# Storing the few first keys at both ends of a key row, one transpose fewer per attention head, and two moves in TensorE's order

## The chip, the cores and the metric

The kernel runs on one core of a Trainium2 chip. Its time is the device time of one execution in microseconds. The kernel before took 1043.29 us, the median of three runs from 1043.16 to 1043.96.

## The reference

One decoder layer over 16 meta tokens and 256 tokens (272 in all) of width 2048, in float32. One product gives eight attention queries of width 128, a shared key and value latent of width 256, sixteen indexer queries of width 64 with one indexer key, and 1024 pooling channels.

```python
score = jnp.einsum('bqhs,bqh->bqs', jax.nn.relu(dots), wi).astype(jnp.float32)
...
_, sel = lax.top_k(score, top_k)
...
logits = jnp.einsum('bqhc,bqkc->bhqk', qa, c_sel).astype(jnp.float32) * (HEAD_DIM ** -0.5)
...
p = jax.nn.softmax(logits, axis=-1).astype(c_sel.dtype)
```

The indexer's score picks the 64 best admissible keys of each query; logits get a relative bias, and the softmax's weights sum the values of those keys. Beside it, four groups of the pooling channels get trailing means over 2, 4, 8 and 16 tokens, less the token, and a small product. Both halves go through one output product, a layer norm, a gated feed-forward part with a short convolution, and a second layer norm.

## The kernel before

TensorE does nearly all of its products in three passes: each float32 operand is split into an upper part in the chip's rounded float32 form and a lower part, and upper times upper, upper times lower and lower times upper are summed (L199 to L201 for the projections). ScalarE makes the upper part of each weight tile (L127), VectorE the lower (L128), SyncE's queue brings the tiles, two ahead.

The 256 queries stand in two blocks of 128. The first block looks at keys 0 to 143 (`KA` = 144), the second at all 272 (`KB`); the two sets lie side by side in rows of `KW` = 416. In both, the 16 meta keys come first. They are the "few first keys", handled apart from the 128 or 256 others: their values are a separate tile `v0` (L419), in which the rows of an upper part, a lower part and the upper part again start at partitions 0, 32 and 64, with cleared rows between.

The order of the work before the output product is this:

1. TensorE warms up on a cleared tile with 13 small products (L86 to L89), then makes indexer keys, weights and latent (L268 to L270).
2. Eight weight tiles make the indexer's queries, a pair of heads each. The pair before is multiplied with the indexer keys in between (`dots`, L352); ScalarE applies the relu (L361, L362) and VectorE adds it to `score` (L364).
3. The key heads (L394 to L401): six products each into one of four PSUM buffers `at`, which `small()` hands out in turn, evacuated by ScalarE (L401). The indexer's last pair is issued behind the third of the eight heads and uses the same buffers.
4. The values (L421 to L438): meta keys first, through `few` (L409), then the two other blocks.
5. The top-k on VectorE (L444 to L448), a comparison that marks the keys left out (L450), and eight updates of the bias (L452). Meanwhile TensorE makes the eight query heads (L456 to L460).
6. The head loop (L585). Each turn computes one tile of pooling channels in 16 groups of three matmuls and puts the attention in between: behind group 4 the logits of the next head (`softmax`), behind group 7 the values of the head before (`values`), behind group 9 the transposes of this head's softmax (`turn`). `turn` makes five transposes: three of 128 keys and, of the two blocks' meta keys, two of 16. `ptx`, the turned weights of the meta keys, is a cleared tile into which ScalarE and VectorE copy upper, upper and lower parts (L514 to L520). Behind the tile, ScalarE evacuates it to `u` (L549), GpSimd adds 4, 4, 3, 3, 2, 2, 1 and 1 times for the window sums (L553), and VectorE takes the token off (L559) in the next turn.

The framework orders each engine's instructions by its own scheduling, within what the program's dependences leave; pools with few buffers make an instruction wait for the reader of the buffer before. After the loop come the output product, the norm and the feed-forward part, which the change doesn't touch.

Of the kernel before, what the change touches and what calls it, by code (L numbers as in the profile page):

```python
# [11 lines left out]
F32 = mybir.dt.float32  # L12
# [5 lines left out]
P = 128  # L18
D = 2048
NM = 16  # L20
# [48 lines left out]
def tile_layer(ctx, tc, xt, w_first, w_proj, w_uk, w_uv, w_pool, w_o, w_up, w_down, cols, rows, rel_bias, onehot, out):  # L69
# [16 lines left out]
    nc.gpsimd.memset(warm, 0.0)  # L86
    ps = small()
    for _ in range(13):
        nc.tensor.matmul(ps[:, :256], warm[:, :P], warm, start=True, stop=True)  # L89


# [200 lines left out]
    ct = kt[:, H - 2:, :]  # L292
    sqs = []
    for j in range(2):
        ps = heads[1 + j][0]
# [37 lines left out]
    def relative_bias():  # L333
        rb_sb = temp([32, H], "rb_sb")
        nc.sync.dma_start(rb_sb, rel_bias)
        oh = temp([32, T], "oh")
        nc.sync.dma_start(oh, onehot)
        ps = small()
        nc.tensor.matmul(ps[:H, :T], rb_sb, oh, start=True, stop=True)
        strip = temp([H, STRIP], "strip")  # L340
        nc.vector.memset(strip, NEG)
        nc.vector.tensor_copy(strip[:, P:], ps[:H, :T])
        strip_d = dram.tile([H, STRIP], F32, name="strip_d")
        nc.gpsimd.dma_start(strip_d, strip)
        for dst, n_rows, t0, n in ((bias[:, :, :KB], P, NM + P, KB), (bias[:, :, KB:], P, NM, KA), (bias_m, 2, Q0, NM)):

            src = bass.AP(tensor=strip_d.tensor, offset=strip_d.offset + P + t0 - (n - 1),
                          ap=[[1, n_rows], [STRIP, H], [1, n]])
            nc.gpsimd.dma_start(dst, src)


    def dots(j, qi, pa_, heads):  # L352

        for i in heads:
            h = 2 * j + i
            pb = small()
            for o, n, t in ((pa_[:, S * i:S * i + S], S, slice(0, P)), (pb[:, :T], T, slice(P, S))):
                nc.tensor.matmul(o, qi[:, i, t], kidx[:, 0, :n], start=True, stop=False)  # L358
                nc.tensor.matmul(o, qi[:, i, t], kidx[:, 1 + i, :n], start=False, stop=True)
# [34 lines left out]
    for h in range(H):  # L394
        ps = small()
        for c in range(2):
            w = slice(1024 * c + h * HD, 1024 * c + h * HD + HD)
            nc.tensor.matmul(ps[:, :T], uk[:, 0, w], ctp[:, c, 0, :], start=c == 0, stop=False)
            nc.tensor.matmul(ps[:, :T], uk[:, 0, w], ctp[:, c, 1, :], start=False, stop=False)
            nc.tensor.matmul(ps[:, :T], uk[:, 1, w], ctp[:, c, 0, :], start=False, stop=c == 1)  # L400
        nc.scalar.activation(kt[:, h, :], ps[:, :T], AF.Copy)  # L401
# [12 lines left out]
    for i, (a, b) in enumerate(((0, NM), (NM, NM + P), (NM + P, T))):  # L414
        if i:
            v = ap_.tile([b - a, 1024], F32, name=f"v{i}", tag=f"v{i}")
        else:

            v = ap_.tile([80, 1024], F32R, name="v0")  # L419
            nc.gpsimd.memset(v.bitcast(F32), 0.0)  # L420
        for g in range(2):  # L421
            ps = small()
            for c in range(2):
                w = slice(1024 * c + 512 * g, 1024 * c + 512 * g + 512)
                if i == 0:
                    nc.tensor.matmul(ps[:48], few[:, c, :], uv[:, 0, w], start=c == 0, stop=False)
                    nc.tensor.matmul(ps[:48], few[:, c, :], uv[:, 1, w], start=False, stop=c == 1)
# [12 lines left out]


# [2 lines left out]
    for r in range(TOPK // 8):  # L444
# [2 lines left out]
            nc.vector.max(m8, src[:, a:b])  # L447
            nc.vector.match_replace(out=work[:, a:b], in_to_replace=m8, in_values=src[:, a:b], imm_value=REPLACED)  # L448
        src = work
    nc.vector.tensor_tensor(work, work, score, op=ALU.is_equal)  # L450
    for h in range(H):
        nc.vector.scalar_tensor_tensor(bias_of(h), work, NEG, bias_of(h), op0=ALU.mult, op1=ALU.add)  # L452


    qt = ap_.tile([P, H, NQ], F32, name="qt", tag="q")
# [11 lines left out]
    lm = ap_.tile([2, H, NM], F32, name="lm")  # L467
# [9 lines left out]
    pm_sb = ap_.tile([NM, H, 2], F32, name="pm_sb")  # L477

    def meta_weights():
        pmeta = small()  # L480
        for h in range(H):
            nc.tensor.transpose(pmeta[:NM, 2 * h:2 * h + 2], lm[:, h, :], ident[:2, :2])
        nc.vector.tensor_copy(pm_sb.rearrange("p a b -> p (a b)"), pmeta[:NM, :2 * H])


    mix = [None] * KT
    AB = ((0, KA), (KA, KW))

    def softmax(h):
        ps = big()  # L490
        nc.tensor.matmul(ps[:, :KA], qt[:, h, 2:2 + P], kt[:, h, :KA], start=True, stop=True)
        nc.tensor.matmul(ps[:, KA:KW], qt[:, h, 2 + P:], kt[:, h, :], start=True, stop=True)
        lg = temp([P, KW], "lg")
        nc.vector.scalar_tensor_tensor(lg, ps[:, :KW], scale, bias_of(h), op0=ALU.mult, op1=ALU.add)
        st = ap_.tile([P, 3, 2], F32, name="st", tag="st", bufs=2)
        for i, (a, b) in enumerate(AB):
# [3 lines left out]
        for i, (a, b) in enumerate(AB):  # L500
            nc.vector.tensor_scalar_mul(lg[:, a:b], lg[:, a:b], st[:, 2, i:i + 1])
        return lg

    def turn(h, lg):
        pt, ptm = small(), small()
        nc.tensor.transpose(pt[:, :P], lg[:, NM:KA], ident)
        nc.tensor.transpose(pt[:, P:2 * P], lg[:, KA + NM:KA + NM + P], ident)
        nc.tensor.transpose(pt[:, 2 * P:3 * P], lg[:, KA + NM + P:], ident)
        nc.tensor.transpose(ptm[:NM, :P], lg[:, :NM], ident)
        nc.tensor.transpose(ptm[:NM, P:2 * P], lg[:, KA:KA + NM], ident)  # L510
        pts = temp([P, 3 * P], "pts")
        nc.scalar.activation(pts, pt[:, :3 * P], AF.Copy)

        ptx = ap_.tile([80, NQ], F32R, name="ptx", tag="t", bufs=4, padded_shape=[P, KW])  # L514
        nc.gpsimd.memset(ptx.bitcast(F32), 0.0)
        for r in (0, 32):
            nc.vector.tensor_copy(ptx[r:r + NM, :2], pm_sb[:, h, :])
            nc.scalar.activation(ptx[r:r + NM, 2:], ptm[:NM, :2 * P], AF.Copy)
        nc.vector.tensor_tensor(ptx[64:64 + NM, :2], pm_sb[:, h, :], ptx[:NM, :2].bitcast(F32), op=ALU.subtract)
        nc.vector.tensor_tensor(ptx[64:64 + NM, 2:], ptm[:NM, :2 * P], ptx[:NM, 2:].bitcast(F32), op=ALU.subtract)  # L520
        return pts, ptx

    def values(h, pts, ptx):
# [61 lines left out]
    for h in range(H):  # L585
# [498 lines left out]
```

## Time and profile before

| | |
|---|---|
| median of three runs | 1043.29 us |
| the profiled execution | 1043.2 us |
| its span, first to last instruction | 1041.3 us |
| granted TensorE clock, mean | 0.998 |
| TensorE, VectorE, ScalarE, GpSimd busy | 1033.3, 891.0, 621.0, 189.5 us |
| DMA, mean | 240 GB/s |

A row of the timeline has the start in microseconds from the span's start, the time that the row takes, the engine (PE is TensorE, PEld its weight loads, DVE VectorE, ACT ScalarE, POOL GpSimd, SP SyncE), the line of the kernel, the operation, what it writes and what it reads, and a count where equal neighbours are put together. In square brackets stands the idle time of the engine ahead of it with what ended that. Matmuls are pipelined: one row lasts longer than the step to the next, so the steps between starts are what tell.

### The profile page before, as it was taken

To read this page: it belongs to the slowest core of one execution; us is meant where nothing else is said; L and a number is where in the kernel's file an instruction comes from. 1 tells how busy PE (TensorE), PEld (TensorE's weight loads), DVE (VectorE), ACT (ScalarE), POOL (GpSimd) and SP (SyncE) were. 2 spreads that over 40 slices of the span, in tenths; PEclk is the share of its full clock that TensorE was granted. 3 is DMA by queue.
4 is the path that set the end of the run, shared out by engine and by line. 5 is a ranking of instruction groups with operands and counts; after the bars stand their busy time and mean duration, and the time that the engine had idled before them with its cause. 6 is when DMAs were issued, how large, how long until landed. Compare 5 with 4: busy or idle time off the path is not lost.

```text
span 1041.3 us, 19198 instructions
## 1 busy us (share of the span) xinstructions
PE 1033.3 (99%) x7643; PEld 984.3 (95%) x7643; DVE 891.0 (86%) x1401; ACT 621.0 (60%) x1000; POOL 189.5 (18%) x246
## 2 busy tenths in 40 slices
PE   9999999999999999999999999999999999999997
PEld 9999999999999999999999999999999999999986
DVE  6879568758779998888999999989998999999876
ACT  7656446645439855555665556555556565565665
POOL 1200014125330021130121111211112101120031
PEclk9999999999999999999999999999999999999999
DMA  9755543354553578879887788877988778887865
GB/s 326 259 187 218 214 142 131 134 200 165 176 189 131 197 223 240 278 282 302 274 277 261 269 297 276 276 263 267 296 271 285 264 274 285 279 273 271 288 215 160
DMA packets 59754, 250.28 MB, mean 240 GB/s; under 512 B 21734, under 2 KB 22416, under 8 KB 32656
## 3 DMA queue, kind: packets, MB, share of 16 engines
q1 hardware_dynamic: 34592, 230.42, 61.2%
q0 software_dynamic: 7888, 16.14, 8.3%
q10 hardware_dynamic: 17184, 2.49, 1.4%
q8 instruction: 60, 0.98, 0.4%
q14 instruction: 30, 0.25, 0.1%
HBM read 232.50 MB, written 2.11 MB: 225 GB/s over the span
## 4 chain that ended last, share of the span: by engine, by line
PE 89%; DVE 5%; issue 3%; ACT 1%; POOL 1%; DMA 1%; POOLq 0%; DVEq 0%; ACTq 0%
PE mm L200 22%; PE mm L199 22%; PE mm L201 22%; PE at L786 6%; PE at L785 6%; PE at L787 6%; DVE whl L128 2%; DMA wraw<-in_w_down 1%; PE mm L268 1%; PE mm L269 1%; PE mm L270 1%; ACT whl L127 1%; DVE x L701 0%; DVE hp L706 0%; PE at L358 0%
## 5 line engine op out<-in xcount | busy, mean ns | idle before, releaser
L128 DVE TENSOR_TENSOR whl<-wraw,whl 128x1024 fp32r<-128x1024 f32 (+1 forms) x416 | 486.3, 1203 | 37.7 <-ACT whl L127 36.8
L127 ACT ACTIVATE whl<-wraw 128x1024 fp32r<-128x1024 f32 (+1 forms) x416 | 402.8, 1015 | 98.6 <-PE mm L201 21.7
L200 PE MATMUL mm<-hp,whl 128*128 128x258 f32 x1280 | 362.4, 283 | 0.1
L199 PE MATMUL mm<-hp,whl 128*128 128x258 f32 x1280 | 361.4, 282 | 0.0
L201 PE MATMUL mm<-hp,whl 128*128 128x258 f32 x1280 | 361.2, 282 | 0.0
L200 PEld LDWEIGHTS mm<-hp,whl 128*128 128x128 f32 x1280 | 242.7, 190 | 3.3 <-DVE hp L706 0.3
L199 PEld LDWEIGHTS mm<-hp,whl 128*128 128x128 f32 x1280 | 242.5, 189 | 3.3
L201 PEld LDWEIGHTS mm<-hp,whl 128*128 128x128 f32 x1280 | 242.9, 190 | 0.2
L199 PE MATMUL mm<-xp,whl 128*128 128x256 f32 (+5 forms) x384 | 111.9, 291 | 0.0
L200 PE MATMUL mm<-xp,whl 128*128 128x256 f32 (+5 forms) x384 | 108.7, 283 | 0.0
L201 PE MATMUL mm<-xp,whl 128*128 128x256 f32 (+5 forms) x384 | 108.7, 283 | 0.0
L720 ACT ACTIVATE z<-mm,cv 128x256 f32<-128x256 f32 x40 | 22.6, 564 | 100.9 <-PE mm L201 100.9
L757 POOL TENSOR_TENSOR forms<-za 128x128 f32<-128x128 f32 x20 | 21.9, 1095 | 309.6 <-DVE za L738 243.1
L720 ACT ACTIVATE za<-mm,cv 128x256 f32<-128x256 f32 x40 | 22.6, 565 | 85.5 <-PE mm L201 77.4
L199 PEld LDWEIGHTS mm<-xp,whl 128*128 128x128 f32 x384 | 72.4, 189 | 1.0 <-issue 0.5
L200 PEld LDWEIGHTS mm<-xp,whl 128*128 128x128 f32 x384 | 72.3, 188 | 0.4
L201 PEld LDWEIGHTS mm<-xp,whl 128*128 128x128 f32 x384 | 72.4, 189 | 0.3 <-DVE whl L128 0.2
L786 PE MATMUL at<-whl,gp 128*128 128x512 f32 x180 | 71.1, 396 | 0.0
L787 PE MATMUL at<-whl,gp 128*128 128x512 f32 x180 | 71.0, 395 | 0.0
L785 PE MATMUL at<-whl,gp 128*128 128x512 f32 x180 | 69.3, 395 | 0.0
L760 POOL TENSOR_TENSOR forms<-za 128x128 f32<-128x128 f32 x20 | 22.6, 1131 | 199.0 <-DVE za L738 185.4
L787 PEld LDWEIGHTS at<-whl,gp 128*128 128x128 f32 x180 | 33.8, 188 | 7.9
(348 smaller groups left out, 1918.2 us busy)
## 6 DMA issues: line engine op xcount, KB each, us to landing
wraw<-in_w_up SPq DMA_DIRECT2D x88, 1024.0 KB, 5.0
wraw<-in_w_down SPq DMA_DIRECT2D x80, 1024.0 KB, 6.2
wraw<-in_w_proj SPq DMA_DIRECT2D x24, 1024.0 KB, 5.1
wraw<-in_w_o SPq DMA_DIRECT2D x16, 1024.0 KB, 4.9
y<-v POOLq DMA_DIRECT2D x27, 256.0 KB, 8.2
y<-u POOLq DMA_DIRECT2D x18, 256.0 KB, 4.9
wraw<-in_w_first SPq DMA_DIRECT2D x8, 304.0 KB, 5.4
x<-in_xt SPq DMA_DIRECT2D x1, 2176.0 KB, 8.4
```

Of the source, the lines that this page charges most:

```text
L127: upper = nc.scalar.activation(hl[:, 0, c], raw[:, c], AF.Copy)
L128: lower = nc.vector.tensor_tensor(hl[:, 1, c], raw[:, c], hl[:, 0, c].bitcast(F32), op=ALU.subtract)
L199: nc.tensor.matmul(ps, wh, ah, start=n == 0, stop=False)
L200: nc.tensor.matmul(ps, wh, al, start=False, stop=False)
L201: nc.tensor.matmul(ps, wl, ah, start=False, stop=n == KT - 1)
L268: nc.tensor.matmul(ps[:m, :T], wh, x_parts[k][:, 0, :], start=k == 0, stop=False)
L720: nc.scalar.activation(z, src[:, 2:NQ], AF.Identity, bias=col(C_B, j), scale=col(C_W, 3 * j + 2))
L757: nc.gpsimd.tensor_tensor(s[:, 0], a21, a22, op=ALU.add)
L760: nc.gpsimd.tensor_tensor(s[:, 3], a11, a21, op=ALU.subtract)
L785: nc.tensor.matmul(ps, a[:, 0, i], hl[:, 0, w], start=j == 0, stop=False)
L786: nc.tensor.matmul(ps, a[:, 0, i], hl[:, 1, w], start=False, stop=False)
L787: nc.tensor.matmul(ps, a[:, 1, i], hl[:, 0, w], start=False, stop=j == n - 1)
```

## The change

The second block's keys are stored from key 16 on, with the meta keys at the end: the key tile gets 16 more columns, a copy of the first 16 (GpSimd), and each row of 416 logits is now 256 others of the second block, its 16 meta keys, the first block's 16 meta keys, its 128 others. The two sets of meta keys are then 32 neighbouring columns, which one transpose turns. Its 32 rows hold both blocks' meta weights for all 128 queries; a mask of one column for each block (`of_block`, made from the identity) sets the rows of the other block to zero as they are copied to `ptx`. `few`, `v0` and `ptx` then have 32 rows for each part, with no cleared rows between. The bias is loaded in three pieces instead of two and the mark of keys left out is written in the new order, by three comparisons.

In TensorE's order the logits of the next head go behind the values of the one before, and the indexer's last pair goes behind the fifth key head, in buffers of the other PSUM pool (`big`). The warm-up reads a constant instead of a cleared tile and has 14 products.

```diff
-    warm = sb.tile([P, 256], mybir.dt.bfloat16, name="warm")
-    nc.gpsimd.memset(warm, 0.0)
+    warm = nc.const_aps.tensor(1.0, (P, 256), mybir.dt.bfloat16)
     ps = small()
-    for _ in range(13):
+    for _ in range(14):
...
-    kt = ap_.tile([P, H, T], F32, name="kt")
+    kt = ap_.tile([P, H, T + NM], F32, name="kt")
...
-        for dst, n_rows, t0, n in ((bias[:, :, :KB], P, NM + P, KB), (bias[:, :, KB:], P, NM, KA), (bias_m, 2, Q0, NM)):
+        for dst, n_rows, t0, s0, n in ((bias[:, :, :KA], P, NM, 0, KA), (bias[:, :, KA:KA + NM], P, NM + P, 0, NM),
+                                       (bias[:, :, KA + NM:], P, NM + P, NM, KB - NM), (bias_m, 2, Q0, 0, NM)):
...
-        if h == 2:
-            dots(7, qis[7], small(), (0, 1))
+        if h == 4:
+            dots(7, qis[7], big(), (0, 1), big)
+    nc.gpsimd.tensor_copy(kt[:, :, T:], kt[:, :, :NM])
...
-    few = ap_.tile([P, 2, 48], F32R, name="few")
-    nc.gpsimd.memset(few.bitcast(F32), 0.0)
-    for p in range(2):
-        nc.gpsimd.tensor_copy(few[:, :, 32 * p:32 * p + NM], ctp[:, :, p, :NM])
+    few = ap_.tile([P, 2, 4, NM], F32R, name="few")
+    for p in range(4):
+        nc.gpsimd.tensor_copy(few[:, :, p, :], ctp[:, :, p // 2, :NM])
...
-            nc.scalar.activation(v[:b - a, w], ps[:b - a], AF.Copy)
-            if i == 0:
-                low = v[32:32 + NM, w]
-                nc.vector.tensor_tensor(low, ps[:NM], v[:NM, w].bitcast(F32), op=ALU.subtract)
-                nc.vector.tensor_tensor(low, ps[32:32 + NM], low.bitcast(F32), op=ALU.add)
-                nc.scalar.activation(v[64:64 + NM, w], ps[:NM], AF.Copy)
+            if i:
+                nc.scalar.activation(v[:, w], ps[:b - a], AF.Copy)
+            else:
+                low = v[32:64, w]
+                nc.scalar.activation(v[:32, w], ps[:32], AF.Copy)
+                nc.gpsimd.tensor_copy(v[64:, w], v[:32, w])
+                nc.vector.tensor_tensor(low, ps[:32], v[:32, w].bitcast(F32), op=ALU.subtract)
+                nc.vector.tensor_tensor(low, ps[32:64], low.bitcast(F32), op=ALU.add)
...
-    nc.vector.tensor_tensor(work, work, score, op=ALU.is_equal)
+    out_of = temp([P, KW], "out_of")
+    for to, a, b in ((0, KA + NM, KW), (KB - NM, KA, KA + NM), (KB, 0, KA)):
+        nc.vector.tensor_tensor(out_of[:, to:to + b - a], work[:, a:b], score[:, a:b], op=ALU.is_equal)
...
+    of_block = ap_.tile([2 * NM, 2], F32, name="of_block")
+    for i in range(2):
+        nc.vector.tensor_reduce(of_block[:, i:i + 1], ident[:2 * NM, NM * i:NM * i + NM], axis=AX.X, op=ALU.add)
...
-        nc.tensor.matmul(ps[:, :KA], qt[:, h, 2:2 + P], kt[:, h, :KA], start=True, stop=True)
-        nc.tensor.matmul(ps[:, KA:KW], qt[:, h, 2 + P:], kt[:, h, :], start=True, stop=True)
+        nc.tensor.matmul(ps[:, KB:KW], qt[:, h, 2:2 + P], kt[:, h, :KA], start=True, stop=True)
+        nc.tensor.matmul(ps[:, :KB], qt[:, h, 2 + P:], kt[:, h, NM:], start=True, stop=True)
...
-        nc.tensor.transpose(ptm[:NM, :P], lg[:, :NM], ident)
-        nc.tensor.transpose(ptm[:NM, P:2 * P], lg[:, KA:KA + NM], ident)
+        nc.tensor.transpose(ptm[:2 * NM, :P], lg[:, 2 * P:2 * P + 2 * NM], ident)
...
-        ptx = ap_.tile([80, NQ], F32R, name="ptx", tag="t", bufs=4, padded_shape=[P, KW])
-        nc.gpsimd.memset(ptx.bitcast(F32), 0.0)
-        for r in (0, 32):
-            nc.vector.tensor_copy(ptx[r:r + NM, :2], pm_sb[:, h, :])
-            nc.scalar.activation(ptx[r:r + NM, 2:], ptm[:NM, :2 * P], AF.Copy)
-        nc.vector.tensor_tensor(ptx[64:64 + NM, :2], pm_sb[:, h, :], ptx[:NM, :2].bitcast(F32), op=ALU.subtract)
-        nc.vector.tensor_tensor(ptx[64:64 + NM, 2:], ptm[:NM, :2 * P], ptx[:NM, 2:].bitcast(F32), op=ALU.subtract)
+        ptx = ap_.tile([96, NQ], F32R, name="ptx", tag="t", bufs=4, padded_shape=[P, KW])
+        blocks = [(slice(2 + P * i, 2 + P * i + P), of_block[:, 1 - i:2 - i]) for i in range(2)]
+        nc.vector.tensor_copy(ptx[:32, :2], pm_sb[:, h, :])
+        for w, keep in blocks:
+            nc.scalar.activation(ptx[:32, w], ptm[:2 * NM, :P], AF.Copy, scale=keep)
+        nc.vector.tensor_copy(ptx[32:64], ptx[:32])
+        nc.vector.tensor_tensor(ptx[64:, :2], pm_sb[:, h, :], ptx[:32, :2].bitcast(F32), op=ALU.subtract)
+        for w, keep in blocks:
+            nc.vector.scalar_tensor_tensor(ptx[64:, w], ptm[:2 * NM, :P], keep, ptx[:32, w].bitcast(F32),
+                                           op0=ALU.mult, op1=ALU.subtract)
...
-        lg_next = softmax(h + 1) if h + 1 < H else None
         product(ps[:, :T - starts[g]], hl, P, x_parts, starts[g], T, k0=4, k1=7)
         if turned:
             values(h - 1, *turned)
+        lg_next = softmax(h + 1) if h + 1 < H else None
         product(ps[:, :T - starts[g]], hl, P, x_parts, starts[g], T, k0=7, k1=9)
```

The meta queries' own softmax (`lm`, L467) is computed in the upper half of a cleared tile of 32 columns, and its transposes write 32 rows in the same way.

More of the change, by code (lines that the diff above doesn't have):

```diff
@@ L344, in relative_bias, with dots @@
         nc.gpsimd.dma_start(strip_d, strip)
-        for dst, n_rows, t0, n in ((bias[:, :, :KB], P, NM + P, KB), (bias[:, :, KB:], P, NM, KA), (bias_m, 2, Q0, NM)):
-            src = bass.AP(tensor=strip_d.tensor, offset=strip_d.offset + P + t0 - (n - 1),
+        for dst, n_rows, t0, s0, n in ((bias[:, :, :KA], P, NM, 0, KA), (bias[:, :, KA:KA + NM], P, NM + P, 0, NM),
+                                       (bias[:, :, KA + NM:], P, NM + P, NM, KB - NM), (bias_m, 2, Q0, 0, NM)):
+            src = bass.AP(tensor=strip_d.tensor, offset=strip_d.offset + P + t0 - s0 - (n - 1),
                           ap=[[1, n_rows], [STRIP, H], [1, n]])
             nc.gpsimd.dma_start(dst, src)
-    def dots(j, qi, pa_, heads):
+    def dots(j, qi, pa_, heads, buffer=small):
         for i in heads:
             h = 2 * j + i
-            pb = small()
+            pb = buffer()
             for o, n, t in ((pa_[:, S * i:S * i + S], S, slice(0, P)), (pb[:, :T], T, slice(P, S))):
@@ L417, in tile_layer @@
         else:
-            v = ap_.tile([80, 1024], F32R, name="v0")
-            nc.gpsimd.memset(v.bitcast(F32), 0.0)
+            v = ap_.tile([96, 1024], F32R, name="v0")
         for g in range(2):
@@ L425, in tile_layer @@
                 if i == 0:
-                    nc.tensor.matmul(ps[:48], few[:, c, :], uv[:, 0, w], start=c == 0, stop=False)
-                    nc.tensor.matmul(ps[:48], few[:, c, :], uv[:, 1, w], start=False, stop=c == 1)
+                    stack = few[:, c].rearrange("p a b -> p (a b)")
+                    nc.tensor.matmul(ps[:64], stack, uv[:, 0, w], start=c == 0, stop=False)
+                    nc.tensor.matmul(ps[:64], stack, uv[:, 1, w], start=False, stop=c == 1)
                     continue
@@ L481, in meta_weights @@
         for h in range(H):
-            nc.tensor.transpose(pmeta[:NM, 2 * h:2 * h + 2], lm[:, h, :], ident[:2, :2])
-        nc.vector.tensor_copy(pm_sb.rearrange("p a b -> p (a b)"), pmeta[:NM, :2 * H])
+            nc.tensor.transpose(pmeta[:2 * NM, 2 * h:2 * h + 2], both_few[:, h, :], ident[:2, :2])
+        nc.vector.tensor_copy(pm_sb.rearrange("p a b -> p (a b)"), pmeta[:2 * NM, :2 * H])
     mix = [None] * KT
-    AB = ((0, KA), (KA, KW))
+    BA = ((0, KB), (KB, KW))
     def softmax(h):
         ps = big()
-        nc.tensor.matmul(ps[:, :KA], qt[:, h, 2:2 + P], kt[:, h, :KA], start=True, stop=True)
-        nc.tensor.matmul(ps[:, KA:KW], qt[:, h, 2 + P:], kt[:, h, :], start=True, stop=True)
+        nc.tensor.matmul(ps[:, KB:KW], qt[:, h, 2:2 + P], kt[:, h, :KA], start=True, stop=True)
+        nc.tensor.matmul(ps[:, :KB], qt[:, h, 2 + P:], kt[:, h, NM:], start=True, stop=True)
         lg = temp([P, KW], "lg")
@@ L495, in softmax @@
         st = ap_.tile([P, 3, 2], F32, name="st", tag="st", bufs=2)
-        for i, (a, b) in enumerate(AB):
+        for i, (a, b) in enumerate(BA):
             nc.vector.tensor_reduce(st[:, 0, i:i + 1], lg[:, a:b], axis=AX.X, op=ALU.max, negate=True)
@@ L499, in softmax @@
         nc.vector.reciprocal(st[:, 2, :], st[:, 1, :])
-        for i, (a, b) in enumerate(AB):
+        for i, (a, b) in enumerate(BA):
             nc.vector.tensor_scalar_mul(lg[:, a:b], lg[:, a:b], st[:, 2, i:i + 1])
@@ L505, in turn @@
         pt, ptm = small(), small()
[L506 to L510, printed above, removed]
+        nc.tensor.transpose(pt[:, :P], lg[:, KB + NM:], ident)
+        nc.tensor.transpose(pt[:, P:2 * P], lg[:, :P], ident)
+        nc.tensor.transpose(pt[:, 2 * P:3 * P], lg[:, P:2 * P], ident)
+        nc.tensor.transpose(ptm[:2 * NM, :P], lg[:, 2 * P:2 * P + 2 * NM], ident)
         pts = temp([P, 3 * P], "pts")
         nc.scalar.activation(pts, pt[:, :3 * P], AF.Copy)
-        ptx = ap_.tile([80, NQ], F32R, name="ptx", tag="t", bufs=4, padded_shape=[P, KW])
-        nc.gpsimd.memset(ptx.bitcast(F32), 0.0)
-        for r in (0, 32):
-            nc.vector.tensor_copy(ptx[r:r + NM, :2], pm_sb[:, h, :])
-            nc.scalar.activation(ptx[r:r + NM, 2:], ptm[:NM, :2 * P], AF.Copy)
-        nc.vector.tensor_tensor(ptx[64:64 + NM, :2], pm_sb[:, h, :], ptx[:NM, :2].bitcast(F32), op=ALU.subtract)
-        nc.vector.tensor_tensor(ptx[64:64 + NM, 2:], ptm[:NM, :2 * P], ptx[:NM, 2:].bitcast(F32), op=ALU.subtract)
+        ptx = ap_.tile([96, NQ], F32R, name="ptx", tag="t", bufs=4, padded_shape=[P, KW])
[8 more added lines that the diff above has]
+                                           op0=ALU.mult, op1=ALU.subtract)
         return pts, ptx
```

12 lines of the change are left out of this document (7 added, 5 removed).

## The prediction

> **What bounds the kernel now.** I read the page first: busy shares, slices, chain.
>
> ```profile
> span 1041.3 us, 19198 instructions
> ...
> PE 1033.3 (99%) x7643; PEld 984.3 (95%) x7643; DVE 891.0 (86%) x1401; ACT 621.0 (60%) x1000; POOL 189.5 (18%) x246
> ...
> PE   9999999999999999999999999999999999999997
> ...
> PEclk9999999999999999999999999999999999999999
> ...
> PE 89%; DVE 5%; issue 3%; ACT 1%; POOL 1%; DMA 1%; POOLq 0%; DVEq 0%; ACTq 0%
> ```
>
> TensorE is busy 1033.3 of 1041.3 us, in every slice, at full clock, and the chain that ended last is 89% TensorE. So a microsecond saved on VectorE, ScalarE, GpSimd or a queue is worth nothing by itself. The time moves in two ways only: a TensorE instruction goes, or TensorE waits more or less. The edits lie before 215 us and TensorE stays busy behind them up to the last slice, so I carry what they give, unchanged, to the end.
>
> Next I read the timeline for where TensorE waits. Its matmuls start every 0.12 to 0.125 us; a longer step is a wait. The largest one that the change touches is at 80 us, between the key heads and the indexer's last pair:
>
> ```profile
> 79.51 1.06 ACT L127 ACTIVATE whl<-wraw 128x1024 fp32r<-128x1024 f32 x1
> 79.61 0.29 PE L400 MATMUL at<-ctp,whl 128*128 128x272 f32 x1
> 79.74 0.28 PE L358 MATMUL at<-kidx,qi 128*128 128x256 f32 x1
> ...
> 79.97 0.28 PE L199 MATMUL mm<-xp,whl 128*128 128x258 f32 x1
> 80.09 0.28 PE L200 MATMUL mm<-xp,whl 128*128 128x258 f32 x1
> ...
> 80.39 0.39 PE L201 MATMUL mm<-xp,whl 128*128 128x258 f32 x1
> 80.59 0.98 ACT L401 ACTIVATE kt<-at 128x272 f32<-128x272 f32 x3
> 80.62 0.28 PE L199 MATMUL mm<-xp,whl 128*128 128x258 f32 x1
> ...
> 81.04 0.39 PE L358 MATMUL at<-kidx,qi 128*128 128x272 f32 x1
> 81.27 0.29 PE L359 MATMUL at<-kidx,qi 128*128 128x272 f32 x1
> ...
> 82.22 0.29 PE L400 MATMUL at<-ctp,whl 128*128 128x272 f32 x1
> ```
>
> From 79.97 to 82.22 TensorE starts 12 matmuls in 2.25 us; at 0.12 each they would take 1.46. So 0.79 us is lost here. The row at 81.04 is released by ScalarE's first key evacuation (80.59 plus a third of 0.98, so 80.92), which frees the PSUM buffer.
>
> **The change part by part.**
>
> *One transpose fewer per head.* Here is one head's turn:
>
> ```profile
> 153.14 0.27 PE L506 MATMUL at<-ident,lg 128*128 128x128 f32 x1
> ...
> 153.47 0.27 PE L509 MATMUL at<-ident,lg 128*16 128x128 f32 x1
> 153.57 0.27 PE L510 MATMUL at<-ident,lg 128*16 128x128 f32 x1
> 153.60 0.37 PE L199 MATMUL mm<-xp,whl 128*128 128x272 f32 x1
> ```
>
> Four steps from 153.14 to 153.57 are 0.43 us, so 0.1075 for one transpose, and the narrow L509 and L510 cost what a wide one does. The new turn has four instead of five: 8 heads x 0.1075 = **-0.86**. No other TensorE work changes: the logits keep their 144 and 272 columns, the value product for the few keys streams the same 258 columns over 96 instead of 80 partitions, and its projection keeps 512 columns.
>
> *The indexer's last pair behind the fifth head.* The key heads use four small PSUM buffers. In the order of the changed program heads 0 to 4 stand together, and the fifth waits for the evacuation of the first, the same one at 80.92. ScalarE's rows ahead of it (the conversion at 79.51) don't move. So the fourth head runs from 79.74 to 80.48, the fifth still starts at 81.04 (0.55 lost) and its second matmul another 0.11 late, as 81.27 was. Then, 12 matmuls on, the second indexer head's last block waits for the relu of the first, which now queues on ScalarE behind the fifth evacuation. The fifth head ends near 82.1; its evacuation takes a third of 0.98, to 82.4, and the relu as much again, to 82.7; TensorE wants it at 82.63 and gets it near 82.8: 0.17, and 0.11 of refill. Together 0.94 against 0.79: **+0.15**. The bounds are -0.79 (no wait at all) and +0.4 (the relu later by one more evacuation, 0.33). I take 0.15, since the releasing row is itself in the trace. Query head 0's four matmuls, which stood in this gap as filling, only move behind the values.
>
> *Logits behind values.* It moves no work off TensorE, and TensorE does not wait at either place now, so nothing is gained. It does move dates: the value product comes ahead of the logits, so it wants its operand `ptx` 0.7 us sooner, and VectorE and ScalarE work in another order. The rows of the second head's loop, up to its value product:
>
> ```profile
> 149.72 3.89 POOL L553 TENSOR_TENSOR win<-win 128x271 f32<-128x271 f32 x3
> 149.83 3.19 DVE L128 TENSOR_TENSOR whl<-wraw,whl 128x1024 fp32r<-128x1024 f32 x2 [0.70 <-ACT whl L127]
> ...
> 152.94 0.58 DVE L494 SCALAR_TENSOR_TENSOR lg<-mm,bias 128x416 f32<-128x416 f32 x1
> ...
> 153.65 0.43 DVE L559 SCALAR_TENSOR_TENSOR diff<-win,u 128x258 f32<-128x258 f32 x1
> ...
> 154.55 0.42 DVE L531 TENSOR_TENSOR mixa<-at,mixa 128x258 fp32r<-128x258 f32 x1
> ...
> 155.68 0.74 ACT L518 ACTIVATE ptx<-at 16x256 fp32r<-16x256 f32 x2
> 156.57 0.41 DVE L520 TENSOR_TENSOR ptx<-at,ptx 16x256 fp32r<-16x256 f32 x1
> 156.78 0.38 ACT L549 ACTIVATE u<-mm 128x272 f32<-128x272 f32 x1
> ...
> 159.62 0.29 PE L526 MATMUL at<-ptx,v 80*128 80x258 f32 x1
> ```
>
> Before, `ptx` is ready at 156.98 and wanted at 159.62: 2.6 us to spare. After, VectorE's `diff` stands ahead of `mixa` and the logits and waits for GpSimd's window sums (to 153.61). Behind it queue `mixa`, the logits' evacuation, the maxima, and so ScalarE's exponentials, its two copies into `ptx`, and `u`, which starts GpSimd's next sums. That closes a ring: diff 0.43, mixa 0.42 and logits 0.58 end at 155.05 instead of 153.52. Maxima and exponentials end near 156.8; two masked copies (unseen on 32 partitions; at most the 0.37 of one in the row above, at least half of it by columns, I take 0.3) at 157.4; one VectorE copy and two subtractions (unseen too; at most the 0.41 of L520, at least half of it, I take 0.28) at 158.2. TensorE arrives at 159.62 - 0.71 - 0.22 + 0.15 = 158.8, so 0.6 to spare. `u` is 0.6 late, so the ring turns in about 8.5 us against TensorE's 7.9 for a head. In the third head `ptx` comes near 166.75 and TensorE near 166.55: **+0.2** (0 to 1.0). The sums are then 3, 2 and 1 additions instead of 4 and the ring catches up.
>
> *Few keys at both ends, bias in new order.* VectorE's top-k starts about 1.1 us later (relu later), but one weight conversion moves behind the eight bias updates:
>
> ```profile
> 44.00 1.87 POOL L349 DMA_DIRECT2D bias<-strip_d  x2 [1.47 <-DMA strip_d<-strip]
> ...
> 83.44 0.65 DVE L447 MAX8 m<-score 128x8 f32<-128x144 f32 x2
> ...
> 87.39 2.34 DVE L128 TENSOR_TENSOR whl<-wraw,whl 128x1024 fp32r<-128x1024 f32 x2
> ...
> 99.57 1.22 DVE L128 TENSOR_TENSOR whl<-wraw,whl 128x1024 fp32r<-128x1024 f32 x1
> ...
> 101.20 1.22 DVE L128 TENSOR_TENSOR whl<-wraw,whl 128x1024 fp32r<-128x1024 f32 x1
> 102.34 4.09 DVE L452 SCALAR_TENSOR_TENSOR bias<-work,bias 128x416 f32<-128x416 f32 x8
> ...
> 104.12 0.28 PE L201 MATMUL mm<-xp,whl 128*128 128x258 f32 x1
> ```
>
> The updates start at 102.34 - 2 x 1.13 + 1.1 + 0.2 (three comparisons for one) = 101.4 and end at 105.4. The second half of query head 2 is then ready at 106.6. TensorE ends head 1 at 104.24, needs that half 24 matmuls later, at 107.1, and at 107.2 with the new wait. Covered, with 0.6 us to spare: 0. GpSimd loses eight clears and gets a key copy and two value copies, beside a VectorE that is not late otherwise: 0. The bias transfers, three instead of two, are issued at 44.00, 57 us before use: 0. SyncE's token load goes one weight later, with no reader near: 0.
>
> *The start.* The warm-up loses its clear:
>
> ```profile
> 1.10 2.95 PE L89 MATMUL at<-warm 128*128 128x256 bf16 x13 [1.10 <-POOL warm L86]
> ...
> 5.96 0.33 PE L270 MATMUL mm<-xp,whl 128*128 128x272 f32 x1
> ...
> 9.20 0.51 DVE L225 TENSOR_TENSOR whl<-wraw,whl 128x336 fp32r<-128x336 f32 x1
> ...
> 9.76 0.35 PE L270 MATMUL mm<-xp,whl 128*80 128x272 f32 x1
> ```
>
> Thirteen in 2.95 us are 0.227 apart; the real ones also step by 0.22 up to 5.96 and by 0.12 later, so the clock opens 4.9 us after the first matmul. Beginning 0.35 sooner may open it 0.35 sooner, worth half: 0.17. But at 9.76 TensorE takes data that VectorE finished at 9.71, so most of that is lost again: **-0.05** (0 to -0.17). The Trainium skill ("TensorE: Matmul & The Clock Gate", the clock gate's table) has the gate look at a free-running window of about 3.4 us, so that the opening need not follow the first matmul; by it the start would move either way by a fraction of a window. The 4.9 us here fit it, but no run shown here shows the window.
>
> Sum: -0.86 + 0.15 + 0.2 - 0.05 = **-0.56**. The profiled execution took 1043.2 (span 1041.3 and 1.9 around it), close to the median of 1043.29; so 1042.6 to 1042.7, and I say **1042.7**.
>
> **The rivals.**
>
> *The ring decides (slower side).* The place is the wait of `diff` on GpSimd ahead of the softmax. At the upper bounds the second, third and fourth heads' values are late by 0.1, 1.0 and 0.2: 1043.2 - 0.86 + 0.15 + 1.3 - 0.05 = 1043.7. It crosses no change from 0.76 us of lateness in all. If the ring doesn't catch up with shorter windows, and seven heads lose 0.5 each, 1046. For it: VectorE's pair takes 3.19 beside GpSimd's sums and 2.34 without, so both are slow exactly there. Against: 2.6 us of slack now, and shorter windows from the third head. Chance 0.2, with 0.08 for the far end.
>
> *The wait at 80 us goes.* Were the fifth head not held by its buffer, 0.94 less: 1041.7; with the start's 0.17 and no late value, 1041.4. For it: five heads are 1.5 us of work for ScalarE to use. Against: it is busy with a conversion to 80.57. Chance 0.12.
>
> *Query head 2 comes late.* GpSimd's new copies fall into VectorE's top-k. The pair above lost 0.85 us beside 3.89 of sums, 0.22 per microsecond; for some 3 us of copies (four small, a key, two value copies, by GpSimd's durations above) that is 0.7, hardly over the 0.6 to spare. If VectorE stood still for all of it, 2.4 us would come out: 1045.0. Chance 0.1, with 0.03 for that end. The Trainium skill ("SBUF — State Buffer", two separate sides) states just that: one of the two holds the shared ports for its whole instruction and the other blocks. The 3.19 for two operations beside 3.89 of sums is less than that full wait, so I give its end little.
>
> *The change does what it should and nothing else is late*: the forecast, 0.58.
>
> **How the numbers follow.** About 0.2% (2.1 us) is what a measurement of this kernel can tell from no change. Faster by that means below 1041.2: all of -0.86, -0.79 and -0.17 come to 1.82, so nearly out of reach, 0.03. Slower means above 1045.4: the far ends of ring and query head, 0.11. Within: 0.86. The range takes the bounds of wait, ring and start: 1041.6 to 1044.3.
>
> **What would show it.** Turns of four transposes 0.1075 apart; a TensorE step near 81 released by the first key evacuation, and about 0.94 us lost there; the second head's value product on time and the third's less than 0.3 late; query head 2 without a step at its middle; data, not clock, at 9.7. The prediction is wrong if TensorE waits for `ptx` in more than two heads, or if the steps at 80 us are gone.

## The result and the profile after

The changed kernel takes 1045.18 us (median of 22 runs, 1044.19 to 1046.87) against 1043.87 of the kernel before (22 runs beside them, 1043.08 to 1045.09). The ratio is 1.0013, with a 95% interval of 1.0007 to 1.0019: slower by 0.7 to 2.0 us. The forecast was 0.6 us faster. (Times here and below are medians; a ratio with its interval is taken over all runs, so it can differ from the quotient of two medians by a few ten-thousandths.)

The page of the changed kernel, the lines that answer to those of before:

```profile
span 1042.8 us, 19178 instructions
...
PE 1034.1 (99%) x7636; PEld 984.4 (94%) x7636; DVE 894.8 (86%) x1413; ACT 618.7 (59%) x998; POOL 185.7 (18%) x242
...
PE 83%; DVE 7%; issue 3%; DMA 2%; POOL 2%; ACT 2%; SPq 0%; POOLq 0%; DVEq 0%; ACTq 0%
```

The shares tell little: TensorE is as busy as before. Only the chain hints that others hold TensorE back: it has 83% of the chain instead of 89%, VectorE 7% instead of 5%, and GpSimd, ScalarE and the DMA 2% each instead of 1%. The place comes out when four marks, which stand at the same point of the work in any version, are read from the timelines: the evacuation of the fifth indexer product, of the first and the last query head, and the first addition behind an output tile. Before:

```profile
57.78 0.38 ACT L383 ACTIVATE qi<-mm 64x256 fp32r<-64x256 f32 x1 [1.08 <-PE mm L201]
98.68 0.39 ACT L460 ACTIVATE qt<-mm 128x258 f32<-128x258 f32 x1 [2.56 <-PE mm L201]
139.12 0.39 ACT L460 ACTIVATE qt<-mm 128x258 f32<-128x258 f32 x1 [3.54 <-PE mm L201]
216.20 0.42 DVE L628 SCALAR_TENSOR_TENSOR x<-x,mm 128x258 f32<-128x258 f32 x1 [0.60 <-PE mm L201]
```

After (L384, L465 and L641 are the same lines of the program):

```profile
58.66 0.38 ACT L384 ACTIVATE qi<-mm 64x256 fp32r<-64x256 f32 x1 [1.09 <-PE mm L200]
99.67 0.39 ACT L465 ACTIVATE qt<-mm 128x258 f32<-128x258 f32 x1 [3.33 <-PE mm L200]
140.11 0.39 ACT L465 ACTIVATE qt<-mm 128x258 f32<-128x258 f32 x1 [3.53 <-PE mm L200]
218.12 0.42 DVE L641 SCALAR_TENSOR_TENSOR x<-x,mm 128x258 f32<-128x258 f32 x1 [0.60 <-PE mm L200]
```

The differences of neighbouring marks, for these two and for the kernels of the next section:

| kernel | up to the 5th indexer product | to the first query head | query heads | head loop | span |
|---|---|---|---|---|---|
| before | 57.78 | 40.90 | 40.44 | 77.08 | 1041.3 |
| after | 58.66 | 41.01 | 40.44 | 78.01 | 1042.8 |
| `old_logits` | 59.94 | 41.02 | 40.44 | 76.30 | 1042.9 |
| `old_dots` | 58.58 | 40.93 | 40.44 | 78.04 | 1043.0 |
| `few_only` | 58.31 | 40.90 | 40.44 | 76.30 | 1040.6 |
| `late_diff` | 59.16 | 41.01 | 40.44 | 76.24 | 1042.5 |
| `logits_only` | 58.65 | 40.90 | 40.44 | 78.11 | 1043.6 |
| `warm_only` | 58.61 | 40.92 | 40.44 | 77.09 | 1041.8 |
| `win4` | 59.24 | 41.03 | 40.44 | 77.86 | 1043.3 |
| `win5` | 58.05 | 41.02 | 40.44 | 77.93 | 1042.4 |
| `spread` | 59.07 | 40.12 | 40.44 | 76.28 | 1040.9 |
| `late_spread` | 58.37 | 40.13 | 40.44 | 76.23 | 1039.8 |

The three middle columns repeat within 0.03 us between kernels that are alike there, so they settle tenths of a microsecond that the times alone can't: an interval of eleven runs is 1.9 us wide. The first column differs by up to 1.6 us between kernels that are alike there, which their edits don't explain (last section), and the stretch behind the loop by up to a microsecond more. So what can be pinned on the change lies in the loop (+0.93) and at 80 us (+0.11): +1.04 together, inside the measured 0.7 to 2.0.

In the loop, the timeline of the changed kernel has two steps where TensorE waits for the operand of a value product (L539), in the third and the fifth head:

```profile
163.31 0.43 DVE L572 SCALAR_TENSOR_TENSOR diff<-win,u 128x258 f32<-128x258 f32 x1 [0.64 <-POOL win L566]
163.65 0.42 DVE L544 TENSOR_TENSOR mixa<-at,mixa 128x258 fp32r<-128x258 f32 x1
163.99 0.58 DVE L505 SCALAR_TENSOR_TENSOR lg<-mm,bias 128x416 f32<-128x416 f32 x1
...
166.27 0.59 ACT L528 ACTIVATE ptx<-at,of_block 32x128 fp32r<-32x128 f32 x2
...
167.48 0.60 DVE L532 SCALAR_TENSOR_TENSOR ptx<-at,of_block,ptx 32x128 fp32r<-32x128 f32 x2
...
168.23 0.36 PE L539 MATMUL at<-ptx,v 96*128 96x258 f32 x1 [0.46 <-ACT whl L126]
```

```profile
177.82 2.78 DVE L127 TENSOR_TENSOR whl<-wraw,whl 128x1024 fp32r<-128x1024 f32 x2
178.04 3.03 POOL L566 TENSOR_TENSOR win<-win 128x263 f32<-128x263 f32 x2 [1.03 <-DVE df L577]
...
181.10 0.43 DVE L572 SCALAR_TENSOR_TENSOR diff<-win,u 128x258 f32<-128x258 f32 x1 [0.51 <-POOL win L566]
...
185.53 0.60 DVE L532 SCALAR_TENSOR_TENSOR ptx<-at,of_block,ptx 32x128 fp32r<-32x128 f32 x2
...
186.28 0.36 PE L539 MATMUL at<-ptx,v 96*128 96x258 f32 x1 [0.83 <-DVE ptx L532]
```

VectorE finishes the operand at 168.08 and at 186.13, and the product follows 0.15 later. (The first product's wait is put down to a weight conversion of ScalarE, which ends at the same 168.08 but which the product doesn't read; in `old_dots` below, whose loop is alike, the same wait is put down to VectorE's `ptx`.) By TensorE's own pace the products would have begun 0.63 and 1.00 us sooner. In both, VectorE's `diff` comes first, waits for GpSimd, and everything of the softmax queues behind it.

### The profile page after: what moved, and what is told of

It reads as the page before. It is cut to its first block, busy times and chain, and to the rows that moved or that the text cites. A ratio compares the mean times of both kernels' runs of the same rounds, so it can differ in the third digit from the quotient of the medians.

```text
span 1042.8 us, 19178 instructions
## 1 busy us (share of the span) xinstructions
PE 1034.1 (99%) x7636; PEld 984.4 (94%) x7636; DVE 894.8 (86%) x1413; ACT 618.7 (59%) x998; POOL 185.7 (18%) x242
## 4 chain that ended last, share of the span: by engine, by line
PE 83%; DVE 7%; issue 3%; DMA 2%; POOL 2%; ACT 2%; SPq 0%; POOLq 0%; DVEq 0%; ACTq 0%
PE mm L199 21%; PE mm L200 21%; PE mm L198 21%; PE at L799 6%; PE at L800 6%; PE at L798 6%; DVE whl L127 3%; POOL win L566 1%; DMA wraw<-in_w_proj 1%; DMA wraw<-in_w_down 1%; ACT whl L126 1%; DVE x L714 0%; DMA wraw<-in_w_first 0%; DVE hp L719 0%; POOL gb L917 0%
## 5 line engine op out<-in xcount | busy, mean ns | idle before, releaser
L770 POOL TENSOR_TENSOR forms<-za 128x128 f32<-128x128 f32 x20 | 21.2, 1062 | 314.2 <-DVE za L751 247.7
L773 POOL TENSOR_TENSOR forms<-za 128x128 f32<-128x128 f32 x20 | 18.9, 945 | 198.8 <-DVE za L751 198.8
```

Source lines behind the costliest of these rows:

```text
L770: nc.gpsimd.tensor_tensor(s[:, 0], a21, a22, op=ALU.add)
L773: nc.gpsimd.tensor_tensor(s[:, 3], a11, a21, op=ALU.subtract)
```

## Experiments

Each kernel below is the changed one with the edit shown, unless it says "before". All times beside the kernel before are of the same chip and hour. The loop is the column "head loop" of the table, the stretch at 80 us the column "to the first query head".

**The logits ahead of the values again.**

```diff
+        lg_next = softmax(h + 1) if h + 1 < H else None
         product(ps[:, :T - starts[g]], hl, P, x_parts, starts[g], T, k0=4, k1=7)
         if turned:
             values(h - 1, *turned)
-        lg_next = softmax(h + 1) if h + 1 < H else None
```

> The changed kernel with one move undone: the next head's logits are issued ahead of the values again. The head loop is measured from the last query head's evacuation to the first output tile's addition: 77.1 us before, 78.0 after. Theory (the move makes VectorE take the window difference ahead of the softmax, and the ring through GpSimd makes the few keys' operand late for the values): without the move the waits of 0.63 and 1.00 us ahead of the third and fifth value products go, the loop takes 76.2 to 76.4, and the time falls by 1.2 to 1.7 against the changed kernel. Rival (the masked copies and the longer VectorE work of the one-transpose form make the operand late in any order): the loop stays at 77.5 or more and a wait ahead of a value product remains. Start: if the late arrival of the second input slice (0.86 us lost by 10 us into the changed kernel's profile) is chance, this run's start may lie anywhere between the two; if the constant warm-up causes it, the same 0.86 stands here.

The loop takes 76.30; no value product waits. The move costs 78.01 - 76.30 = 1.71 us, and the one-transpose form alone is not late. The time was 1043.03 against 1043.51 before, ratio 0.9999 (0.9990 to 1.0008), against the changed kernel's 1.0013: by the ratios 1.5 us less, as the theory said, though the intervals meet. The loop's column is what shows it.

**The indexer's last pair behind the third key head again.**

```diff
-        if h == 4:
-            dots(7, qis[7], big(), (0, 1), big)
+        if h == 2:
+            dots(7, qis[7], small(), (0, 1))
```

> The changed kernel with the indexer's last pair behind the third key head again, in the small buffers. Theory: only the stretch around 80 us changes, by 0.1 to 0.2 us less; the head loop keeps its 78.0 and the time falls by 0 to 0.3. Rival (the later top-k, by 1.1 us, is what makes the head loop late): the loop falls below 77.5 too.

The second column falls by 0.08 and the loop stays at 78.04: this move costs a tenth of a microsecond, and it has nothing to do with the loop. Ratio 1.0011 (1.0002 to 1.0020).

**The few keys alone**: both edits above together.

> Only the new storing of the few keys with its one transpose: both moves undone, the warm-up kept on its constant (the cleared tile finds no room beside the longer key tile). Theory: a head loop of 76.2 to 76.4 (eight transposes of 0.11 less than before), and a time 0.4 to 0.9 below the kernel before unless the stretch at the very end gives some of it back. Rival (the new copies cost more than the transposes save): loop 77.1 or more and no gain.

The loop takes 76.30, so 0.78 us less than before, and 1042.65 us against 1043.51: ratio 0.9993 (0.9984 to 1.0002). In the loop, the new storing of the few keys gains what it should; the time agrees, but could not tell it from nothing alone.

**The window difference behind the softmax's maxima.** The logits stay behind the values; only VectorE's order changes (`maxima` holds the reduction of L508):

```diff
         if mean:
-            less_token(*mean)
+            m = maxima[min(h + 1, H - 1)]
+            with tc.issue_after(getattr(m, "ins", m)):
+                less_token(*mean)
```

> The changed kernel with one thing added: VectorE's window difference is ordered behind the maxima of the next head's softmax. Theory (the difference that stands ahead of the softmax and waits for GpSimd is the cause): the logits are evacuated about 0.9 us sooner, the waits ahead of the third and fifth value products go, loop 76.2 to 76.6, time down by 1.1 to 1.7 against the changed kernel. Rival (the values simply come 0.7 us too soon, whatever VectorE's order): the loop stays above 77.5.

Here is the third head's stretch in this kernel's timeline (its rows stand 0.5 us later than the changed kernel's, by the mark behind the query heads):

```profile
162.03 0.42 DVE L545 TENSOR_TENSOR mixa<-at,mixa 128x258 fp32r<-128x258 f32 x1
...
162.37 0.57 DVE L506 SCALAR_TENSOR_TENSOR lg<-mm,bias 128x416 f32<-128x416 f32 x1
...
163.61 0.41 DVE L573 SCALAR_TENSOR_TENSOR diff<-win,u 128x258 f32<-128x258 f32 x1
...
165.58 0.60 DVE L533 SCALAR_TENSOR_TENSOR ptx<-at,of_block,ptx 32x128 fp32r<-32x128 f32 x2
...
168.10 0.28 PE L540 MATMUL at<-ptx,v 96*128 96x258 f32 x1
```

The logits are evacuated 1.6 us sooner (162.37 instead of 163.99), even though this profile runs 0.5 later, `diff` finds GpSimd done, and the operand is ready at 166.18, 1.9 us ahead of its product. The loop takes 76.24: the whole 1.7 us is gone with one VectorE instruction of each turn in another place, with the values as early as in the change. Ratio 0.9995 (0.9986 to 1.0004).

**The kernel before with the logits' move alone** (the reverse of the first edit).

> The kernel before with one move alone: the logits behind the values, five transposes and cleared tiles as before. Theory (the move alone puts the window difference ahead of the softmax and makes the values wait): the loop from the last query head's evacuation to the first output tile grows from 77.1 to 78.2 to 78.8, and the time is 1 to 1.7 slower than before. Rival (only together with the new copies does it get late): loop 77.1 to 77.3, time as before.

The loop grows to 78.11, by 1.03, just short of the 78.2 expected. The theory holds: the move alone makes TensorE wait. But it costs 1.03 here and 1.71 beside the one-transpose form, so that form takes part in the lateness, and the waits are not the two from above. The fifth value product is 0.26 late, and in the last head this row is the largest:

```profile
204.27 0.27 PE L508 MATMUL at<-ident,lg 128*128 128x128 f32 x1
204.33 0.48 DVE L577 SCALAR_TENSOR_TENSOR mixp<-at,cv,mixp 128x258 fp32r<-128x258 f32 x1
...
204.87 0.28 PE L509 MATMUL at<-ident,lg 128*16 128x128 f32 x1 [0.33 <-DVE mixp L577]
```

The fourth transpose there waits for VectorE's pooled product. So the late VectorE shows wherever TensorE next needs it. Ratio 1.0008 (0.9999 to 1.0017), which by itself would not tell it from no change.

**The kernel before with the new warm-up alone.**

```diff
-    warm = sb.tile([P, 256], mybir.dt.bfloat16, name="warm")
-    nc.gpsimd.memset(warm, 0.0)
+    warm = nc.const_aps.tensor(1.0, (P, 256), mybir.dt.bfloat16)
     ps = small()
-    for _ in range(13):
+    for _ in range(14):
```

> The kernel before with only the warm-up changed, on the constant and with 14 products. Theory (the start differs from run to run by when the input slices arrive): time within 0.4 us of before, the third indexer product's evacuation anywhere between 57.7 and 60. Rival (the constant warm-up itself makes the start late): about 0.8 slower.

1043.59 against 1043.68, ratio 1.0001 (0.9992 to 1.0010): no difference that can be measured, though anything between 0.8 us faster and 1.0 slower is left open.

**Four, then five window buffers.** With four, the room comes from the top-k's working tile, with five also from the tile of ones:

```diff
-        return ap_.tile([P, T + 2], F32, tag="w", name=name, bufs=3)
+        return ap_.tile([P, T + 2], F32, tag="w", name=name, bufs=4)
...
-    work = ap_.tile([P, KW], F32, name="work")
+    work = temp([P, KW], "work")
```

> The changed kernel with four window buffers instead of three; for the room, the top-k's working tile uses a buffer of the temporaries. Theory (in the fifth head GpSimd's second addition waits about 1 us for a window buffer that VectorE's window difference and lower part still read, and this carries the ring on into the fifth head): the wait of 1.00 us ahead of the fifth value product goes or shrinks below 0.3, the one of 0.63 ahead of the third stays, and the loop takes 77.0 to 77.3. Rival (the ring is late there by its own length, and the buffer only shows it): the loop stays at 78.0.

A miss: the loop is 77.86, the fifth head still waits 0.80, and the ratio is 1.0010 (1.0001 to 1.0019). GpSimd's wait had moved to its third addition. Hence five, on top of that edit, in one execution:

```diff
-        return ap_.tile([P, T + 2], F32, tag="w", name=name, bufs=4)
+        return ap_.tile([P, T + 2], F32, tag="w", name=name, bufs=5)
...
-    ones = sb.tile([P, P], F32, name="ones")
-    nc.vector.memset(ones, 1.0)
+    ones = nc.const_aps.tensor(1.0, (P, P), F32)
```

> The changed kernel with five window buffers (with four, the wait of GpSimd only moved from its second to its third addition). For the room, the top-k's working tile uses a buffer of the temporaries and the tile of ones is read from a constant. Theory (the buffer carries the lateness into the fifth head): GpSimd's additions run without a wait there, the wait ahead of the fifth value product goes, loop 77.0 to 77.3, the third's 0.63 stays. Rival (the ring's own length carries it): the fifth keeps 0.6 or more, loop 77.7 to 78.0.

```profile
176.56 1.71 POOL L565 TENSOR_TENSOR win<-win 128x263 f32<-128x263 f32 x2
176.95 0.84 DVE L576 TENSOR_TENSOR df<-diff,df 128x258 fp32r<-128x258 f32 x1
...
177.72 2.77 DVE L127 TENSOR_TENSOR whl<-wraw,whl 128x1024 fp32r<-128x1024 f32 x2
...
180.41 0.42 DVE L571 SCALAR_TENSOR_TENSOR diff<-win,u 128x258 f32<-128x258 f32 x1
```

Now GpSimd runs without a wait and is done at 178.27, two microseconds before `diff`. The loop is still 77.93. The buffer theory falls. The rival's number comes true, but not as it was put: in the fifth head nothing waits for GpSimd any more, so the ring isn't what holds it there. VectorE itself is late: its two weight conversions begin 38.2 us after the last query head's evacuation (139.51 here), as in the changed kernel (177.82 - 140.11 = 37.7), against 35.8 in the kernel with `diff` moved back (176.41 - 140.61). The time that VectorE had lost by the third head's loop is still missing here. The same rows can be followed through the fourth head, in the changed kernel and with `diff` moved back:

```profile
175.10 0.60 DVE L532 SCALAR_TENSOR_TENSOR ptx<-at,of_block,ptx 32x128 fp32r<-32x128 f32 x2
```

```profile
173.42 0.60 DVE L533 SCALAR_TENSOR_TENSOR ptx<-at,of_block,ptx 32x128 fp32r<-32x128 f32 x2
```

From the query heads' mark these are 34.99 and 32.81, so VectorE is 2.2 us late there; it was 2.4 late at the same rows of the third head (27.37 and 24.97), and `diff` does not wait in the fourth. That it is a backlog rests on these offsets and on the runs that cured both waits (`late_diff`, `old_logits`); no run removed the earlier wait alone.

**A version to beat both.** The logits stand ahead of the values (the first edit of this section), and the key heads and the indexer's last pair use both PSUM pools:

```diff
     for h in range(H):
-        ps = small()
+        ps = big() if h == 4 else small()
...
-            dots(7, qis[7], big(), (0, 1), big)
+            dots(7, qis[7], big(), (0,), big)
+            dots(7, qis[7], big(), (1,), small)
```

> A version meant to beat both: the changed kernel with the logits ahead of the values again, and the fifth key head and the indexer's last pair spread over both PSUM pools so that no matmul there waits for an evacuation of the one just before (the fifth head and three of the pair's four blocks in the big buffers, the last block in a small one). Theory (the 0.9 us lost at 80 us is only the wait for a buffer): the stretch from the fifth indexer product to the first query head falls from 40.9 to 40.1 to 40.3, the loop stays at 76.3, time 1.3 to 1.7 below before. Rival (another wait, for the relu or the weights, comes in its place): the stretch stays above 40.6.

The changed kernel's stretch at 80 us, from its timeline:

```profile
81.25 0.28 PE L401 MATMUL at<-ctp,whl 128*128 128x272 f32 x1
81.47 1.27 ACT L402 ACTIVATE kt<-at 128x272 f32<-128x272 f32 x4
...
81.92 0.39 PE L399 MATMUL at<-ctp,whl 128*128 128x272 f32 x1 [0.39 <-ACT kt L402]
82.15 0.29 PE L400 MATMUL at<-ctp,whl 128*128 128x272 f32 x1
...
83.39 0.29 PE L360 MATMUL mm<-kidx,qi 128*128 128x272 f32 x1
...
83.62 0.39 PE L359 MATMUL mm<-kidx,qi 128*128 128x256 f32 x1
83.84 0.28 PE L360 MATMUL mm<-kidx,qi 128*128 128x256 f32 x1
```

And the same in the new version:

```profile
81.66 0.28 PE L401 MATMUL at<-ctp,whl 128*128 128x272 f32 x1
81.78 0.29 PE L399 MATMUL mm<-ctp,whl 128*128 128x272 f32 x1
81.88 1.27 ACT L402 ACTIVATE kt<-at 128x272 f32<-128x272 f32 x4
...
82.89 0.29 PE L360 MATMUL mm<-kidx,qi 128*128 128x272 f32 x1
...
83.01 0.28 PE L359 MATMUL mm<-kidx,qi 128*128 128x256 f32 x1
```

In the changed kernel the fifth head starts 0.67 after the matmul before it, and the second indexer head's 256 columns (L359) 0.23 after theirs; in the new one both start 0.12 after. The stretch falls to 40.12, the loop is 76.28, and the time is 1041.74 against 1043.68: ratio 0.9983 (0.9974 to 0.9992). By the ratio to the kernel before, no kernel here with more than one run is faster.

**The same with the logits behind the values and `diff` moved back**: the edit of `late_diff` on top of it, with the first edit undone.

> The version with the key heads spread over both pools, here with the logits behind the values as in the change, and the window difference ordered behind the softmax's maxima. Theory (the logits' place is worth nothing to TensorE once no value waits): loop 76.2 to 76.3 and stretch at 80 us 40.1, as with the logits ahead of the values. Rival (the later place spares TensorE the switch between kinds of matmul): loop below 76.0.

Loop 76.23, stretch 40.13, one execution of 1041.56 against 1043.11: so once nothing waits, the place of the logits is worth 0.05 us at most, hardly more than the 0.03 by which equal loops differ.

## Why the prediction was wrong

- **One transpose fewer, -0.86**: right in kind. The loop of the few keys alone is 0.78 shorter.
- **The pair behind the fifth head, +0.15**: right, and at the rows that it named. 0.55 and 0.11 lost at the fifth head, 0.11 and 0.10 at the relu, 0.87 in all against 0.94 forecast; the mark shows +0.11, and undoing it takes 0.08 back.
- **Logits behind values, +0.2 (0 to 1.0)**: the step that failed; it is 1.71. The ring was found, with its place (`diff` ahead of the softmax, waiting for GpSimd) and the head where it first shows. The unseen operations were priced well: 0.30 for each masked copy and subtraction, 0.28 for the copy, against 0.3 and 0.28. But the third head came out at 0.63 rather than 0.2 late: the operand was ready 0.34 later than summed, and the 0.15 between VectorE's end and the product was left out of the sum. And then the sentence "the ring catches up" was wrong. I let the lateness end as soon as GpSimd had fewer additions to make. It had gone into VectorE's queue by then. The fourth head's product was on time, for TensorE has twelve pooled products more to do in that turn (172.06 to 173.51), and the operand, ready at 175.70, had until 177.52. But VectorE has two pooled products and a weight split of the map more there (175.74 to 177.55), so it caught up little, and the lateness came out again in the fifth head as 1.00 us.
- **Query head 2 and GpSimd's copies, 0**: right; the query heads take 40.44 in every kernel.
- **The start, -0.05**: no difference that can be measured. TensorE did begin 0.32 sooner and in this profile reached full pace sooner (5.58 instead of 5.96), but then it waited for the input's second slice, at 6.25. The forecast had data decide too, but at 9.7, where the changed kernel shows no longer step; and its pace that follows the first matmul by 4.9 us was one profile's chance (last section).
- **The tail**: the forecast carried a gain "unchanged, to the end". From the last mark on, spans differ by up to a microsecond between kernels that are alike there, so a tenth gained is not seen in one span.

The rival with the ring was the one that happened, at another price: 1043.7 was worked out for the "upper bounds", with 1.3 us of lateness and a fourth head that is late too, and the far end of 1046 has seven heads late by 0.5. It was two heads, by 0.63 and 1.00 and what follows each. Two is also as many as the forecast allowed before it would call itself wrong, so that sign did not show; the third head, 0.63 late where less than 0.3 was named, did. With the measured terms the sum is -0.78 + 0.11 + 1.71 = +1.04.

## What to carry to other kernels

When a step is moved in one engine's program, read the new order on the engines that serve it: an instruction there that waits for a slow third engine holds back everything behind it, and here one VectorE instruction of each turn cost 1.7 us that a better place gave back whole. Lateness that an almost full engine has once taken on need not end with its cause, as the fifth head shows: follow its queue to the next place where it can idle, and look there for the next product that needs it. And where several buffers of one pool hold a stretch back, spread the outputs over another pool before reordering the work: that alone was worth 0.8 us here.

## What the runs showed of the hardware

How long the start takes differs from run to run, and the edits don't set it. One part is when the input's slices land. In the changed kernel's profile:

```profile
0.78 3.14 PE L88 MATMUL at<-const-bfloat16-1.0 128*128 128x256 bf16 x14 [0.78 <-PEq L1086]
...
5.39 0.43 ACT L221 ACTIVATE xp<-wraw 128x272 fp32r<-128x272 f32 x1 [1.35 <-DMA wraw<-in_w_first]
...
6.25 0.35 PE L267 MATMUL mm<-xp,whl 128*80 128x272 f32 x1 [0.26 <-ACT whl L222]
```

The same slice's conversion began at 4.87 in the profile before. The other part is when TensorE goes over from steps of 0.23 us to steps of 0.12. Here are `old_dots` and then `old_logits`, whose first matmuls both start at 0.78:

```profile
4.26 0.29 PE L268 MATMUL mm<-xp,whl 128*80 128x272 f32 x1
4.38 0.28 PE L267 MATMUL mm<-xp,whl 128*128 128x272 f32 x1
```

```profile
9.82 0.43 PE L268 MATMUL mm<-xp,whl 128*128 128x272 f32 x1
10.05 0.34 PE L269 MATMUL mm<-xp,whl 128*128 128x272 f32 x1
10.23 0.29 PE L267 MATMUL mm<-xp,whl 128*128 128x272 f32 x1
```

The first is at full pace by 4.26, 3.5 us behind its first matmul, the second from 10.23, 9.4 us behind; the other profiles lie between them. So the pace does not open at a fixed time behind the first matmul. (The profile's granted clock reads full in both stretches; only the steps show the half pace.) `old_logits` also has the latest fifth indexer product of all, at 59.94. But `old_dots` with the earliest full pace is only at 58.58, for its third slice lands late: either part can decide. Over the twelve profiles the mark lies between 57.78 and 59.94, with the old warm-up at 57.78 and 58.65 and with the new one at 58.05 to 59.94; two profiles of the old one are too few to tell the two warm-ups apart by this mark. The width is near the scatter of 2 to 3 us between runs of one kernel, though only profiles show where a run lost it.

VectorE's two conversions and GpSimd's two additions, beside each other in the fifth head's loop of the changed kernel, take 3.25 us from 177.82 to 181.07. An addition of nearly this size took 0.62 in the same profile where VectorE stood idle:

```profile
194.96 0.62 POOL L566 TENSOR_TENSOR win<-win 128x259 f32<-128x259 f32 x1 [0.43 <-DVE df L577]
195.61 0.43 DVE L572 SCALAR_TENSOR_TENSOR diff<-win,u 128x258 f32<-128x258 f32 x1 [0.80 <-POOL win L566]
```

A pair of conversions alone took 2.34, so one after the other they would take 3.58. That is near to taking turns. The forecast had judged the pair against GpSimd's own drawn-out time and made the sharing look milder than it is. The Trainium skill ("SBUF — State Buffer", two separate sides) has one of the two hold the shared ports for its whole instruction while the other is blocked; these rows agree with it within ten per cent.
